# Key-key and query-key products of the first phase: plain fp32 products of 128 columns, or split products of 256

## The chip, the core and the metric

The kernel runs on one core of a Trainium2 chip. TensorE multiplies, VectorE and ScalarE work element by element, GpSimd does a few small things, and SyncE issues all DMAs of this kernel. The metric is the device time of one execution in microseconds, as the median of several runs. A profile is of one execution of its own, whose time stands beside it below.

## The reference

One layer of a hybrid backbone: 128 context tokens and 2048 latent tokens of 1024 features, thus 17 tiles of 128 tokens. The part that matters here is the front of the mixer, a gated DeltaNet with 4 heads of 128 features:

```python
proj = h @ w_in_l
qkv = jax.nn.silu(centred_conv(qkv, conv_l))
q, k, v = jnp.split(qkv, 3, axis=-1)
q = l2norm(q.reshape(B, T, H_A, DK))
k = l2norm(k.reshape(B, T, H_A, DK))
...
a_mat = jnp.where(strict, jnp.einsum('bnhcd,bnhsd->bnhcs', k_beta, k) * decay, 0.0)
...
qk = jnp.einsum('bnhcd,bnhsd->bnhcs', q, k) * decay
```

For each tile and head, k times k and q times k are needed, both 128 x 128, in fp32 accuracy. The scan over the chunks, the gMLP half, the output projection and the MLP follow.

## The kernel before

The program is written in phases. The first one (about the first 437 us) makes the normalised and modulated rows, projects them to q, k and v, convolves, and leaves in DRAM what the second phase (the scans and the gMLP, to about 1180 us) reads. The rest is the MLP.

The first phase walks over six blocks of tiles, five of three tiles and one of two (`BLOCKS`, line 28). In each block there are twelve feature tiles: k, q and v for each of four heads. The loop that begins with `for n, (gi, h) in enumerate(order)` gives each feature tile one slot. The main work of a slot is eight steps of `project`: three matmuls each, on the high and low parts of weights and rows (`mm3`, lines 241 to 243, 386 columns in most blocks). Between them `interleave` puts the side work of the slot, among it:

- `convolve` (lines 568 to 578), which leaves the features in the tile `x2`;
- `to_tokens` (lines 584 to 607), which transposes a feature tile; for k it also normalises the rows to `kn`, and for v it copies them to `tk`;
- `to_features` (line 614), which transposes `kn` back to `kTt`;
- `products` (lines 619 to 630), once for each head and block, three slots after the later one of its k and q tiles; 24 calls in all;
- steps of the modulation of later layers' parts (`mod_steps`), and of the next block's preparation (`prep_block`).

A matrix product that must be as exact as fp32 is done in one of two ways here. The plain way is a matmul on fp32 operands, which the program issues as two instructions (in the profile, 136 instructions stand for 68 products). The split way rounds each operand to the reduced type `F32R` (high part), takes the difference from it (low part), and adds up three matmuls: high with high, high with low and low with high. `products` uses the plain way before, `project` the split way.

Two things set the order of the work. The program's order gives each instruction a priority; a scheduler then lays out each engine's instructions in advance, from estimated times, so that an instruction whose inputs or buffers are not expected yet is passed by. On the chip each engine then runs its own list strictly as it was laid out. All stores and loads go through the one queue of SyncE.

Buffers come from pools. Tiles of one tag share as many buffers as `bufs` says, of the size of the largest; a new tile waits until the oldest is no longer used. The tags that the change touches: `first` holds the sums of the modulation (`mod_sum`, line 353, used four times in the first 40 us and read by the transposes of `mod_out`, line 361); `tk` holds `tk`, `kn` and, before, `ev`, the copy of the products out of PSUM; `xh` holds ten rows at the borders of blocks, read in the first 27 us. PSUM results of `to_tokens`, `to_features` and `products` share the three banks of `pt`.

Of the kernel before, what the change touches and what calls it, by code (L numbers as in the profile page):

```python
# [8 lines left out]
F32 = mybir.dt.float32  # L9
F32R = mybir.dt.float32r  # L10
# [3 lines left out]
ALU = mybir.AluOpType  # L14
# [3 lines left out]
P = 128  # L18
# [46 lines left out]
def hybrid_step(  # L65
# [7 lines left out]
    V, A, G, T = nc.vector, nc.scalar, nc.gpsimd, nc.tensor  # L73
    load = nc.sync.dma_start
    store = nc.sync.dma_start
# [10 lines left out]
    def f32(ap):  # L86
        return ap.bitcast(F32)
# [12 lines left out]
    kk_d = dp.tile([NT, P, H, P], F32, name="kk_d")  # L100
    qk_d = dp.tile([NT, P, H, P], F32, name="qk_d")
# [6 lines left out]
    def by_tiles(dst, tiles):  # L108

        return dst[tiles].rearrange("a p d -> p a d")  # L110
# [126 lines left out]
    def mm3(ps, trip, first=True, last=True, more=False):  # L237

        n = len(trip)
        for i, (lh, ll, rh, rl) in enumerate(trip):  # L240
            T.matmul(ps, lh, rh, start=first and i == 0, stop=False, skip_group_check=more)  # L241
            T.matmul(ps, lh, rl, start=False, stop=False, skip_group_check=more)  # L242
            T.matmul(ps, ll, rh, start=False, stop=last and i == n - 1, skip_group_check=more)  # L243
# [51 lines left out]
    with ExitStack() as ph:  # L295
        p1 = ph.enter_context(tc.tile_pool(name="p1", bufs=2, reuse_waits="tile"))
        pf = ph.enter_context(tc.tile_pool(name="p1f", bufs=2, reuse_waits="tile"))
# [6 lines left out]
        def pt():  # L304
            return ppt.tile([P, 512], F32, tag="pt", name="pt", bufs=3)
# [7 lines left out]
        for d in range(2):  # L313
            m = p1.tile([P, P], F32, tag=f"mcum{d}", name=f"mcum{d}", bufs=1)
# [9 lines left out]
        st_ = smp.tile([P, 16], F32, tag="c16", name="c16")  # L324
# [23 lines left out]
        def mod_sum(raws, psum):  # L348

            pm = psum()  # L350
            for k in range(KT):
                T.matmul(pm[0:2, :], scond[:, k, :], raws[k], start=k == 0, stop=k == KT - 1)
            row = pf.tile([2, 512], F32, tag="first", name="first", bufs=2)
            A.copy(row, pm[0:2, :])
            return row

# [52 lines left out]
        xh = pf.tile([P, D], F32, tag="xh", name="xh", bufs=1)[0:10, :]  # L409
# [7 lines left out]
        ps = pt()  # L417
# [4 lines left out]
        for t in BLOCKS[0]:  # L422
            x = p1.tile([P, D], F32, tag="x", name="x", bufs=3)
# [120 lines left out]
        def feature_tile(blk, bi, gi, h):  # L544

            hH, hL, ncol, segs = blk
            tiles = BLOCKS[bi]
            nt = len(tiles)
            n = nt * P
            c0 = tiles[0] * P  # L550
            j = gi * 4 + h
            u = {}

            def project(k):
                if k == 0:
                    u["ps"] = (pt if bi == 0 and j == 6 else pj)()
                wh, wl = W1[gi][k]
                mm3(u["ps"][:, :ncol], [(wh[:, h * P : (h + 1) * P], wl[:, h * P : (h + 1) * P],
                                         hH[k][:, :ncol], hL[k][:, :ncol])], first=k == 0, last=k == KT - 1)
                if k == KT - 1:  # L560
                    convolve()

            def convolve():
                ps = u["ps"]
                cv = pf.tile([P, 384], F32, tag="cv", name="cv", bufs=2)
                u["x2"] = x2 = pf.tile([P, 384], F32, tag="x2", name="x2", bufs=4)
                for s, o, m, _ in segs:
                    A.activation(cv[:, o : o + m], ps[:, s : s + m], AF.Copy, scale=convw[:, 1, j : j + 1])  # L568
                for s, o, m, _ in segs:
                    for w, sh in ((0, -1), (2, 1)):  # L570
                        V.scalar_tensor_tensor(out=cv[:, o : o + m], in0=ps[:, s + sh : s + sh + m],  # L571
                                               scalar=convw[:, w, j : j + 1], in1=cv[:, o : o + m],
                                               op0=ALU.mult, op1=ALU.add)
                A.activation(x2[:, :n], cv[:, :n], AF.Tanh, scale=0.5)
                V.scalar_tensor_tensor(out=x2[:, :n], in0=x2[:, :n], scalar=1.0, in1=cv[:, :n], op0=ALU.add,
                                       op1=ALU.mult)
                if gi == 0:
                    store(out=by_tiles(qT_d[:, :, h, :], slice(tiles[0], tiles[0] + nt)),
                          in_=x2[:, :n].rearrange("p (a d) -> p a d", d=P))

            def to_tokens():
                pq = pt()
                for i in range(nt):
                    T.transpose(pq[:, i * P : (i + 1) * P], u["x2"][:, i * P : (i + 1) * P], ident)  # L584
                rows = slice(c0, c0 + n)
                if gi == 2:
                    tk = pf.tile([P, 3, P], F32, tag="tk", name="tk", bufs=4)
                    A.copy(tk[:, :nt, :], pq[:, :n].rearrange("p (a b) -> p a b", b=P))
                    store(out=vt_d[rows, h * P : (h + 1) * P].rearrange("(a p) d -> p a d", p=P),
                          in_=tk[:, :nt, :])  # L590
                    return
                junk = p1.tile([P, P], F32, tag="junk2", name="junk2", bufs=1)
                if gi == 0:
                    for i, t in enumerate(tiles):
                        A.activation(junk, pq[:, i * P : (i + 1) * P], AF.Square,
                                     accum_out=ssq[:, t, h : h + 1])
                    return
                ss = smp.tile([P, 3], F32, tag="ss3", name="ss3")
                rk = smp.tile([P, 3], F32, tag="rk", name="rk")
                for i in range(nt):  # L600
                    A.activation(junk, pq[:, i * P : (i + 1) * P], AF.Square, accum_out=ss[:, i : i + 1])  # L601
                rsqrt_cols(rk[:, :nt], ss[:, :nt], nt, 1.0, 4 * EPS)
                u["kn"] = kn = pf.tile([P, 3, P], F32, tag="tk", name="kn", bufs=4)
                for i in range(nt):
                    A.activation(kn[:, i, :], pq[:, i * P : (i + 1) * P], AF.Copy, scale=rk[:, i : i + 1])
                store(out=kt_d[rows, h * P : (h + 1) * P].rearrange("(a p) d -> p a d", p=P),
                      in_=kn[:, :nt, :])

            def to_features():

                u["kTt"] = kTt = pf.tile([P, 384], F32, tag="kTt", name="kTt", bufs=3)
                pk = pt()
                for i in range(nt):
                    T.transpose(pk[:, i * P : (i + 1) * P], u["kn"][:, i, :], ident)
                V.tensor_copy(kTt[:, :n], pk[:, :n])
                store(out=by_tiles(kT_d[:, :, h, :], slice(tiles[0], tiles[0] + nt)),
                      in_=kTt[:, :n].rearrange("p (a d) -> p a d", d=P))

            def products(q):

                kTt = u["kTt"]
                for dst, rhs in ((kk_d, kTt), (qk_d, q["x2"])):
                    ps = pt()
                    for i in range(nt):
                        T.matmul(ps[:, i * P : (i + 1) * P], kTt[:, i * P : (i + 1) * P],  # L625
                                 rhs[:, i * P : (i + 1) * P], start=True, stop=True)
                    ev = pf.tile([P, 3, P], F32, tag="tk", name="ev", bufs=4)
                    A.copy(ev[:, :nt, :], ps[:, : nt * P].rearrange("p (a b) -> p a b", b=P))
                    store(out=dst[tiles[0] : tiles[0] + nt, :, h, :].rearrange("a p d -> p a d"),
                          in_=ev[:, :nt, :])  # L630

            u["main"] = [lambda k=k: project(k) for k in range(KT)]
            u["to_tokens"] = to_tokens
            u["to_features"], u["products"] = to_features, products
            return u
# [156 lines left out]
        for bi in range(len(BLOCKS)):  # L792
# [8 lines left out]
            for n, (gi, h) in enumerate(order):  # L801
                u = us[n] if bi == 0 and n < 3 else feature_tile(blk, bi, gi, h)
# [157 lines left out]
    with ExitStack() as ph:  # L960
# [465 lines left out]
        for i, u in enumerate(units):  # L1426
            w = p2 if i <= NT else p3
# [7 lines left out]
            n = len(u["prep"])  # L1435
# [6 lines left out]
            if i >= NT:  # L1442
                at(i, lambda u=u: o_loads(u))
                first, second = o_steps(u)
# [76 lines left out]
    def bank():  # L1521
        return psq.tile([P, 512], F32, tag="f", name="f", bufs=8)
# [356 lines left out]
    tiles = {n: [] for n in range(8)}  # L1879
# [49 lines left out]
    for j, t in enumerate(range(8, -1, -1)):  # L1929
        st = h2_steps(t, bank, lambda: w512("junk"), w512)  # L1930
        p = 10 + 19 * j // 2
# [7 lines left out]
    for p, (o, n, b) in enumerate(seq):  # L1939
        u = units[n]  # L1940
# [27 lines left out]
    for m, (n, i, u, q) in enumerate(todo):  # L1968
# [6 lines left out]
        if q == 0:  # L1975
            ps = bank()
# [6 lines left out]
        h, lo = sops.pop(m)  # L1983
        if m >= len(todo) - 4:
# [8 lines left out]
            if q == 3:  # L1993
                rest[0](ps, 0)
                ps = bank()
# [75 lines left out]
```

## Time and profile before

| | |
|---|---|
| runs | 2576.24, 2578.61, 2585.0 us; median 2578.61 |
| profiled execution | 2580.59 us, of it a span of 2578.7 us |
| TensorE's granted clock | 0.997 of full |
| plain products, line 625 | 272 matmul instructions, 38.3 us busy with overlap |
| copies of them, line 628 | 48 on ScalarE, 21.6 us |
| stores of them, line 629 | 48, of 192 KB (128 KB in the last block) |

The page of the profile gives the busy time of each engine and the chain of work that ended last. The views by windows, by lines and by time are answers of the same trace. Matmuls overlap: one may last 0.28 us though the next starts after 0.12. What a matmul costs is therefore read from the distance of starts, or from the chain, where each is charged only up to the next.

### The profile page before, as it was taken

The numbers are of one execution on the slowest core, as the hardware profiler recorded it, in microseconds if no ns is written. First come the engines' busy times: TensorE is split into PE (matmuls) and PEld (weight loads), VectorE is DVE, ScalarE is ACT, GpSimd is POOL, SyncE is SP. The second block draws the span as 40 slices with busy tenths as digits, with TensorE's granted clock in tenths as the row PEclk, the third lists the DMA queues.
The fourth block names the chain that finished last, engine by engine and source line by source line (L and its number), as shares of the span: only waits on it lengthen the run. The fifth ranks groups of instructions, "written<-read, shape, count | busy, mean of one in ns | idle before, by whom it ended". The sixth has DMA issues, their size and how long they took to land.

```text
span 2578.7 us, 44496 instructions
## 1 busy us (share of the span) xinstructions
PE 2539.4 (98%) x15268; PEld 2139.2 (83%) x15268; DVE 1836.7 (71%) x3790; ACT 1259.7 (49%) x3119; POOL 234.2 (9%) x448
## 2 busy tenths in 40 slices
PE   9999999999999999999999999999999999999998
PEld 5999999788888787778888888888888888888887
DVE  5867757776677878886677876777675557685875
ACT  4755556555555667764355543544442433243442
POOL 3112212111111111210000000000000000000000
PEclk9999999999999999999999999999999999999999
DMA  8967737644454657885768789666579979786683
GB/s 293 307 209 216 209 111 256 225 158 153 145 156 159 214 165 243 277 274 176 281 204 257 231 270 358 194 181 188 148 248 370 331 273 330 259 259 205 221 264 113
DMA packets 503912, 588.66 MB, mean 228 GB/s; under 512 B 36148, under 2 KB 298588, under 8 KB 500102
## 3 DMA queue, kind: packets, MB, share of 16 engines
q1 hardware_dynamic: 503686, 585.82, 69.6%
q8 instruction: 120, 1.97, 0.3%
q14 instruction: 106, 0.87, 0.1%
HBM read 406.01 MB, written 179.67 MB: 227 GB/s over the span
## 4 chain that ended last, share of the span: by engine, by line
PE 89%; DMA 5%; DVE 4%; ACT 1%; issue 1%; POOL 0%; SPq 0%; POOLq 0%; DVEq 0%; ACTq 0%
PE f L241 17%; PE f L242 17%; PE f L243 17%; PE pj L241 7%; PE pj L243 7%; PE pj L242 7%; PE pd L1010 5%; PE pm L241 1%; PE pm L243 1%; PE pm L242 1%; DMA raw<-in_w_mod_dram 1%; PE pt L625 1%; PE pt L584 1%; PE pd L1093 1%; DMA hop_d<-opL 1%
## 5 line engine op out<-in xcount | busy, mean ns | idle before, releaser
L241 PE MATMUL f<-hop,zH 128*128 128x512 f32 (+1 forms) x976 | 376.2, 386 | 1.2 <-ACT zH L1531 1.2
L242 PE MATMUL f<-hop,zH 128*128 128x512 f32 (+1 forms) x976 | 376.1, 386 | 0.0
L243 PE MATMUL f<-hop,zL 128*128 128x512 f32 (+1 forms) x976 | 376.1, 386 | 0.0
L241 PE MATMUL f<-hop,wH 128*128 128x512 f32 x896 | 349.7, 391 | 0.6 <-ACT p L1604 0.6
L242 PE MATMUL f<-hop,wH 128*128 128x512 f32 x896 | 348.7, 389 | 0.0
L243 PE MATMUL f<-hop,wL 128*128 128x512 f32 x896 | 347.5, 389 | 0.0
L1531 ACT CAST zH<-zraw 128x512 fp32r<-128x512 f32 x240 | 146.9, 620 | 302.4 <-DMA zraw<-s_d 93.6
L241 PEld LDWEIGHTS f<-hop,zH 128*128 128x128 f32 x976 | 183.3, 188 | 38.6 <-ACT zH L1531 1.6
L243 PEld LDWEIGHTS f<-hop,zL 128*128 128x128 f32 x976 | 183.3, 188 | 37.3 <-DVE zL L1525 0.4
L242 PEld LDWEIGHTS f<-hop,zH 128*128 128x128 f32 x976 | 183.3, 188 | 36.9 <-issue 0.2
L1525 DVE TENSOR_TENSOR zL<-zraw,zH 128x512 fp32r<-128x512 f32 x240 | 163.2, 687 | 66.5 <-ACT zH L1531 54.0
L241 PEld LDWEIGHTS f<-hop,wH 128*128 128x128 f32 x896 | 168.2, 188 | 36.5 <-ACT p L1604 1.7
L243 PEld LDWEIGHTS f<-hop,wL 128*128 128x128 f32 x896 | 168.2, 188 | 35.3
L242 PEld LDWEIGHTS f<-hop,wH 128*128 128x128 f32 x896 | 168.3, 188 | 34.5
L241 PE MATMUL pj<-kH,wH 128*128 128x386 f32 (+2 forms) x568 | 190.5, 338 | 1.3 <-ACT junk L601 1.1
L243 PE MATMUL pj<-kH,wL 128*128 128x386 f32 (+2 forms) x568 | 189.7, 335 | 0.0
L242 PE MATMUL pj<-kL,wH 128*128 128x386 f32 (+2 forms) x568 | 189.5, 335 | 0.1
L184 POOL TENSOR_TENSOR r<-rsq,nhalf 128x1 f32<-128x1 f32 (+1 forms) x37 | 25.7, 694 | 1409.0 <-DVE rsq L183 1409.0
L571 DVE SCALAR_TENSOR_TENSOR cv<-pj,vec,cv 128x384 f32<-128x384 f32 (+2 forms) x164 | 87.0, 539 | 53.4 <-ACT cv L568 52.0
L1531 ACT CAST wH<-s 128x512 fp32r<-128x512 f32 x96 | 59.4, 621 | 124.6 <-DVE s L1525 118.3
L241 PEld LDWEIGHTS pj<-kH,wH 128*128 128x128 f32 x568 | 107.1, 189 | 4.4 <-issue 2.4
L202 DVE TENSOR_TENSOR wL<-raw,wH 128x512 fp32r<-128x512 f32 x120 | 81.7, 688 | 40.0 <-ACT wH L201 36.6
(418 smaller groups left out, 5806.9 us busy)
## 6 DMA issues: line engine op xcount, KB each, us to landing
zraw<-z_d SPq DMA_DIRECT2D x212, 256.0 KB
raw<-in_w_ff_dram SPq DMA_DIRECT2D x192, 256.0 KB
hop<-hop_d SPq DMA_DIRECT2D x28, 1024.0 KB
z_d<-c SPq DMA_DIRECT2D x96, 256.0 KB
zraw<-s_d SPq DMA_DIRECT2D x96, 256.0 KB
raw<-in_w_mod_dram SPq DMA_DIRECT2D x80, 256.0 KB
r<-in_w_ff_dram SPq DMA_DIRECT2D x80, 256.0 KB
s_d<-s SPq DMA_DIRECT2D x64, 256.0 KB
```

The costliest lines, as they stand in the source:

```text
L184: G.tensor_tensor(out=out, in0=t[:np_, :n], in1=nhalf[:np_, :n], op=ALU.pow)
L202: V.tensor_tensor(out=lo, in0=raw, in1=f32(h), op=ALU.subtract)
L241: T.matmul(ps, lh, rh, start=first and i == 0, stop=False, skip_group_check=more)
L242: T.matmul(ps, lh, rl, start=False, stop=False, skip_group_check=more)
L243: T.matmul(ps, ll, rh, start=False, stop=last and i == n - 1, skip_group_check=more)
L571: V.scalar_tensor_tensor(out=cv[:, o : o + m], in0=ps[:, s + sh : s + sh + m], scalar=convw[:, w, j : j + 1], in1=cv[:, o : o + m], op0=AL ...
L584: T.transpose(pq[:, i * P : (i + 1) * P], u["x2"][:, i * P : (i + 1) * P], ident)
L625: T.matmul(ps[:, i * P : (i + 1) * P], kTt[:, i * P : (i + 1) * P], rhs[:, i * P : (i + 1) * P], start=True, stop=True)
L1010: T.matmul(p[:, h, :], lhs[:, h, :], rhs[:, h, :], start=True, stop=True)
L1093: T.matmul(py[:, h], u["X"][:, h, :], pm[:, h], start=True, stop=True)
L1525: V.tensor_tensor(out=out, in0=a, in1=b, op=op)
L1531: A.copy(h, src)
```

## The change

`products` changes from the plain to the split way, and the moving operand of a tile now holds k's columns and q's columns together, 256 in all. The high parts of both go into one tile `kqH` (under the tag `xh`), made on ScalarE; the low parts go into `kqL`, made on VectorE, which takes the buffer of tag `first`. For each tile of tokens, the stationary operand is the high part of k (twice) and its low part (once). Two tiles of tokens fill one PSUM bank, so a call on three tiles uses one bank of 512 columns and one of 256, as against two banks of 384. One copy per bank brings them to `ev`, a tile of its own with one buffer that holds both results of the call; then come the two stores. The row tag `first` and the tag `tk` each lose one buffer (2 to 1 and 4 to 3).

```diff
-            row = pf.tile([2, 512], F32, tag="first", name="first", bufs=2)
+            row = pf.tile([2, 512], F32, tag="first", name="first", bufs=1)
...
-                    tk = pf.tile([P, 3, P], F32, tag="tk", name="tk", bufs=4)
+                    tk = pf.tile([P, 3, P], F32, tag="tk", name="tk", bufs=3)
...
-                u["kn"] = kn = pf.tile([P, 3, P], F32, tag="tk", name="kn", bufs=4)
+                u["kn"] = kn = pf.tile([P, 3, P], F32, tag="tk", name="kn", bufs=3)
...
             def products(q):
 
-                kTt = u["kTt"]
-                for dst, rhs in ((kk_d, kTt), (qk_d, q["x2"])):
+                hi = pf.tile([P, 2, 384], F32R, tag="xh", name="kqH", bufs=1)
+                lo = pf.tile([P, 2, 384], F32R, tag="first", name="kqL", bufs=1)
+                for w, x in enumerate((u["kTt"], q["x2"])):
+                    A.copy(hi[:, w, :n], x[:, :n])
+                    V.tensor_tensor(out=lo[:, w, :n], in0=x[:, :n], in1=f32(hi)[:, w, :n], op=ALU.subtract)
+                ev = pf.tile([P, 2, 3, P], F32, tag="ev", name="ev", bufs=1)
+                for i0 in range(0, nt, 2):
+                    m = min(2, nt - i0)
                     ps = pt()
-                    for i in range(nt):
-                        T.matmul(ps[:, i * P : (i + 1) * P], kTt[:, i * P : (i + 1) * P],
-                                 rhs[:, i * P : (i + 1) * P], start=True, stop=True)
-                    ev = pf.tile([P, 3, P], F32, tag="tk", name="ev", bufs=4)
-                    A.copy(ev[:, :nt, :], ps[:, : nt * P].rearrange("p (a b) -> p a b", b=P))
-                    store(out=dst[tiles[0] : tiles[0] + nt, :, h, :].rearrange("a p d -> p a d"),
-                          in_=ev[:, :nt, :])
+                    for i in range(m):
+                        c = slice((i0 + i) * P, (i0 + i + 1) * P)
+                        out = ps[:, i * 256 : i * 256 + 256].rearrange("p (w d) -> p w d", w=2)
+                        for j, (st_, mv) in enumerate(((hi, hi), (hi, lo), (lo, hi))):
+                            T.matmul(out, st_[:, 0, c], mv[:, :, c], start=j == 0, stop=j == 2)
+                    A.copy(ev[:, :, i0 : i0 + m, :].rearrange("p w a d -> p a w d"),
+                           ps[:, : m * 256].rearrange("p (a w d) -> p a w d", a=m, w=2))
+                for w, dst in enumerate((kk_d, qk_d)):
+                    store(out=dst[tiles[0] : tiles[0] + nt, :, h, :].rearrange("a p d -> p a d"), in_=ev[:, w, :nt, :])
```

## The prediction

> **What bounds the kernel now.** I began with the page, whose busy shares and chain of waits name the engine that sets the end.
>
> ```profile
> span 2578.7 us, 44496 instructions
> PE 2539.4 (98%) x15268; PEld 2139.2 (83%) x15268; DVE 1836.7 (71%) x3790; ACT 1259.7 (49%) x3119; POOL 234.2 (9%) x448
> PE 89%; DMA 5%; DVE 4%; ACT 1%; issue 1%; POOL 0%; SPq 0%; POOLq 0%; DVEq 0%; ACTq 0%
> ```
>
> TensorE is on 89% of the chain. But the change touches only the first phase (up to about 437 us), so the second view is the table of windows, in stretches that follow the blocks of that phase.
>
> ```profile
> core 0: us, PE busy (x) PEld busy (x) DVE busy (x) ACT busy (x) POOL busy (x), PEclk, DMA share, GB/s
> 40.00:110.00 70.00, 68.01 (x403) 65.27 (x401) 55.41 (x141) 49.92 (x140) 18.03 (x42) 1.00 0.88 281
> 110.00:175.00 65.00, 64.05 (x418) 62.16 (x418) 51.15 (x99) 39.73 (x128) 5.44 (x13) 1.00 0.86 267
> 175.00:240.00 65.00, 65.00 (x408) 62.77 (x408) 42.77 (x85) 35.20 (x108) 13.06 (x33) 1.00 0.65 189
> 240.00:300.00 60.00, 60.00 (x387) 57.73 (x386) 44.16 (x89) 33.12 (x103) 11.85 (x37) 1.00 0.68 202
> 300.00:365.00 65.00, 65.00 (x413) 63.26 (x412) 41.08 (x83) 33.08 (x104) 12.98 (x37) 1.00 0.53 153
> 365.00:440.00 75.00, 75.00 (x543) 71.80 (x542) 47.70 (x130) 43.81 (x131) 18.50 (x21) 1.00 0.66 200
> sum 400.00, PE 397.06 PEld 382.99 DVE 282.27 ACT 234.86 POOL 79.85; mean PE 66.18 PEld 63.83 DVE 47.05 ACT 39.14 POOL 13.31
> ```
>
> From 175 us on TensorE never stops: what it is given there is what the phase takes, and a microsecond of matmul removed is a microsecond gained. Before 175 us it stops for 2.94 us (70.00 - 68.01 and 65.00 - 64.05), with the DMA engines at 0.88 and VectorE at 55.41 of 70. A finer set of windows shows where VectorE is full:
>
> ```profile
> 90.00:100.00 10.00, 10.00 (x67) 9.78 (x66) 8.00 (x18) 6.20 (x21) 0.38 (x1) 1.00 1.02 312
> 100.00:110.00 10.00, 10.00 (x61) 9.72 (x59) 7.08 (x16) 7.38 (x19) 6.99 (x30) 1.00 1.01 323
> 110.00:120.00 10.00, 9.05 (x61) 8.60 (x61) 9.97 (x19) 6.10 (x23) 0.44 (x4) 1.00 1.06 351
> ```
>
> From 90 us the DMA engines are full, and from 110 to 120 us VectorE has nothing left. The first block's products fall just here.
>
> **TensorE's sum.** The old products are 24 calls (6 blocks by 4 heads). A call has two products of 128 columns for each tile, and each is two instructions. The view by line and form counts them; the chain gives what each call really costs, because there each matmul is charged only until the next can start.
>
> ```profile
> L625 PE MATMUL pt<-kTt 128*128 128x128 f32 x136 | 19.2, 275 | 0.8 <-ACT junk L595 0.8
> L625 PE MATMUL pt<-x,kTt 128*128 128x128 f32 x136 | 19.1, 275 | 0.0
> 233.36 1.34 PE pt L625 x12
> 413.26 0.89 PE pt L625 x8
> ```
>
> A call on three tiles costs 1.34 us, on two tiles 0.89 us (0.112 us an instruction, not the 275 ns that one of them lasts: they overlap). 20 x 1.34 + 4 x 0.89 = 30.4 us.
>
> The new call has per tile three matmuls with 256 moving columns of the reduced type (high with high, high with low, low with high): 9 or 6 instead of 12 or 8. Such matmuls are the last ones of the kernel, 17 in a row, of which the first and the last:
>
> ```profile
> 2569.72 0.28 PE L242 MATMUL f<-hop,zH 128*128 128x256 f32 x1
> 2571.64 0.28 PE L243 MATMUL f<-hop,zL 128*128 128x256 f32 x1
> ```
>
> 16 steps in 1.92 us: 0.120 us each. 20 x 9 x 0.120 + 4 x 6 x 0.120 = 24.5 us. **TensorE saves 30.4 - 24.5 = 5.9 us**, 0.23% of the time. It is little because a plain fp32 product of 128 columns takes 2 x 0.112 = 0.223 us, while its share of three 256-column matmuls takes 3 x 0.120 / 2 = 0.180 us.
>
> The Trainium skill puts this differently: "TensorE: Matmul & The Clock Gate" (Back-to-back issue gap) gives N / 2.4 + 2.5 ns, 109 ns for 256 columns. By that, as an estimate, the new matmuls would take 22.2 us and the saving would be 8.1 us. The rows above show 120 ns in this kernel, and I go by them.
>
> One form the trace does not have: the moving operand is two runs of 128 columns, 384 apart. It could cost as little as the unbroken row (0.120 us), and at the far end as much per column as the plain products (0.447 us for 256 columns, four times 0.112). I take 0.120, since it has the type and width of that row and differs only by one jump.
>
> **ScalarE and VectorE.** Their new work is not on the chain, but TensorE now has to wait for it.
>
> ```profile
> L628 ACT COPY ev<-pt 128x384 f32<-128x384 f32 x40 | 18.7, 481 | 15.5 <-PE pt L625 14.4 <-DMA kk_d<-ev 0.8 <-DMA qk_d<-ev 0.2
> L628 ACT COPY ev<-pt 128x256 f32<-128x256 f32 x8 | 2.9, 372 | 0.5 <-PE pt L625 0.4
> L201 ACT CAST wH<-raw 128x512 fp32r<-128x512 f32 x51 | 30.5, 633 | 7.9 <-DMA raw<-in_w_in_dram 4.6 <-DMA raw<-in_w_mod_dram 3.2
> L202 DVE TENSOR_TENSOR wL<-raw,wH 128x512 fp32r<-128x512 f32 x50 | 33.3, 682 | 4.2 <-ACT wH L201 3.6 <-PE pj L243 0.3
> L520 DVE TENSOR_TENSOR kL<-full,kH 128x256 fp32r<-128x256 f32 x8 | 3.3, 418 | 0.0
> ```
>
> - Evictions: two of 384 columns become one of 512 and one of 256 (481 + 109 = 590 and 372 ns, the slope from the first two rows). 962 ns before and after; on the last block one of 590 for two of 372. Nothing to speak of.
> - High parts: two casts a call on ScalarE. From the cast of 512, less 109 ns, 0.52 us for 384 columns: 40 x 0.52 + 8 x 0.42 = 24 us.
> - Low parts: two subtractions a call on VectorE. Midway between 418 and 682 ns, 0.55 us: 40 x 0.55 + 8 x 0.42 = 25 us.
>
> Over 40 to 440 us VectorE goes from 282 to 308 of 400 (77%), ScalarE from 235 to 259 (65%). In sum there is room: TensorE's stream covers both. If that cover is gone, a call costs up to its whole preparation, two casts and the last subtraction, 0.52 + 0.52 + 0.55 = 1.6 us.
>
> The inputs are old: k's transposed tile and q's features are made well ahead of the call, since a call is put three tiles after its later one. So the casts can run early; but the single buffers for high and low let them start only when the call before has ended. The chain shows calls 4.5 us apart (233.36 above and the next two), so 4.5 - 1.1 = 3.4 us stay for the 1.6 us of preparation.
>
> ```profile
> 237.87 1.34 PE pt L625 x12
> 242.38 1.34 PE pt L625 x12
> ```
>
> **Moved and shared.** The stores stay 48, of the same size, but both of a call leave after the second eviction, from one buffer, and the next call's first eviction waits until both have landed. The trace shows one such store on the chain, at the end of the phase:
>
> ```profile
> 437.60 4.79 DMA vt_d<-tk
> ```
>
> 4.79 us for a store in full traffic against 4.5 us between calls: the eviction can be late by about 1 us where DMA is full. Queued behind it on ScalarE are the copies, tanh and squares of the next tile; ScalarE is idle 35% of the time, and TensorE has three PSUM banks for these results, so I cost it at nothing; uncovered it is at most 1 us on the calls of the two blocks before 175 us, some 8 us. On SP's queue a waiting store holds back the loads behind it in the same way as now; the first store of a call moves back by about 0.4 us of matmuls and the second eviction. The three buffers left to kn and tk lose one and are rid of 48 of 96 users: nothing. The modulation rows, now one buffer:
>
> ```profile
> 11.87 0.58 ACT L354 COPY first<-pm 2x512 f32<-2x512 f32 x1 [9.06 <-PE pm L352]
> 19.16 0.57 ACT L354 COPY first<-pj 2x512 f32<-2x512 f32 x1 [6.72 <-PE pj L352]
> 16.05 0.41 PE L361 MATMUL pm<-ident,first 2*128 2x2 f32 x4
> 24.20 0.41 PE L361 MATMUL pm<-ident,first 2*128 2x2 f32 x4
> 28.44 0.56 ACT L354 COPY first<-pj 2x512 f32<-2x512 f32 x1
> ```
>
> Each copy already comes after the transposes that read the row before it (19.16 after 16.46, 28.44 after 24.61): one buffer costs nothing.
>
> **What of the saving is kept.** In the first block it meets a transfer that does not come earlier:
>
> ```profile
> 99.04 5.34 DMA raw<-in_w_mod_dram
> 110.98 0.94 PE L625 MATMUL pt<-kTt 128*128 128x128 f32 x6 [0.81 <-ACT junk L595]
> ```
>
> The chain leaves TensorE for a load at 99 us and comes back with a wait of 0.81 us. What its four calls save, 4 x 0.26 = 1.0 us, I take as lost. For new waits on high or low parts I take one more of that 0.81 us, its bounds being none and 24 x 1.6 = 38 us; it lies near none because the phase after 175 us shows not one stop, although transposes there read VectorE's results too. **-5.9 + 1.0 + 0.8 = about -4.0 us**: 2580.6 (the profiled execution: its span and 1.9 us around it) becomes 2576.6. It lies 2.0 us above the median of the runs, 2578.6; so the forecast for the median is **2574.6 us**.
>
> **The rivals.**
> - *Faster, 2568 us (0.20).* The instructions of each engine stand in an order that is laid out from estimated times, so the phase behind can come out in another order. It has slack worth having:
>
> ```profile
> 496.56 4.76 DMA S<-in_state_delta_dram
> 501.46 2.50 PE pd L1010 x16
> 524.88 1.78 PE pd L1010 x16
> ```
>
> TensorE stops for the state's load and then runs 16 matmuls in 2.50 us that later take 1.78. If the load came early, 4.76 + 0.72 = 5.5 us go as well, and with all of the 5.9 kept the sum is -11 us. Against it: nothing in the change aims there, and such luck has two signs.
> - *All of it eaten, 2577 to 2584 us (0.14).* ScalarE's or VectorE's queue is late in the first two blocks only (windows at 9.97 of 10): 8 calls x 0.8 to 1.2 us is 6.4 to 9.6 us against 5.9, or the late stores above.
> - *Slower, 2592 us (0.16).* TensorE waits for the low parts at every call: the subtraction stands in VectorE's queue behind convolutions and modulation sums. The price is that of the wait at 110.98 us: 24 x 0.81 = 19.4, less 5.9, +13.5 us. It decides for slower by more than 0.3% from a mean wait of (5.9 + 7.7) / 24 = 0.57 us a call. For it: VectorE at 79% before 175 us; against it: 3.4 us of room for 1.6 us. The Trainium skill, "TensorE: Matmul & The Clock Gate" (its table's row on queue depth), says that ScalarE and VectorE take their instructions strictly in order; that speaks for this rival, and the wait above, for squares that other squares held back, agrees.
> - *It does not do what it says:* the broken moving operand runs at the far end, 204 x 0.447 = 91 us, +61 us, 2639 us. Only as a share of the slower cases (0.02 of the 0.16), for the reason above.
>
> **How the numbers follow.** The forecast's own case (from the full -5.9 to about -1) has 0.50. 0.3% is 7.7 us, about what a measurement can tell from no change here; so it and the eaten case are "same", 0.64; faster 0.20, slower 0.16. For 8 in 10 the range takes in half of the faster case, to 2567, and reaches half way into the slower one, to 2588.
>
> **What would show it.** Right: the line of the products takes about 1.1 us a call in the chain (x9, or x6 and x3), the windows after 175 us have TensorE full over a shorter stretch, about 1 us less a block. Wrong: waits on the high or low parts in the list of waits of TensorE; a step of the new matmuls above 0.13 us; evictions waiting for stores with TensorE idle behind them; or a second phase whose own span differs by more than 2 us, which no term here covers.

## The result and the profile after

| | before | after |
|---|---|---|
| median of the runs (22 each) | 2578.93 us (2575.43 to 2585.0) | 2584.22 us (2578.08 to 2591.23) |
| profiled execution | 2580.59 us, span 2578.7 | 2582.28 us, span 2580.5 |
| TensorE's granted clock, mean of the runs | 0.9984 (29 other runs of before, those of the first group) | 0.9961 |

The ratio is 1.0021, with an interval of 1.0014 to 1.0028: the change makes the kernel 5.3 us **slower**. It lies inside the range and within 0.3%, but the forecast was 4 us faster. The two profiled executions are only 1.7 us apart, since before's lies above the median of its runs and after's below; the medians decide, and the table's last line will help to say why.

The page of the kernel after, its span, busy times and chain:

```profile
span 2580.5 us, 44424 instructions
PE 2534.8 (98%) x15200; PEld 2133.4 (83%) x15200; DVE 1857.9 (72%) x3838; ACT 1273.0 (49%) x3163; POOL 242.0 (9%) x448
PE 82%; DMA 7%; DVE 6%; ACT 2%; SPq 1%; issue 1%; POOL 0%; POOLq 0%; DVEq 0%; ACTq 0%
```

TensorE is busy 4.6 us less than before (2539.4), and yet the span is longer: time went from matmuls into waits, and the chain has more DMA and DVE than it had. The table of windows says where:

```profile
40.00:110.00 70.00, 68.14 (x401) 65.33 (x399) 57.99 (x147) 51.16 (x145) 18.96 (x33) 1.00 0.87 273
110.00:175.00 65.00, 61.12 (x368) 59.17 (x368) 53.42 (x106) 38.98 (x127) 8.14 (x18) 0.95 0.81 250
175.00:240.00 65.00, 65.00 (x412) 62.79 (x411) 48.44 (x97) 36.50 (x108) 13.70 (x37) 1.00 0.69 198
...
365.00:440.00 75.00, 75.00 (x540) 72.03 (x539) 54.02 (x143) 47.17 (x138) 17.16 (x21) 1.00 0.66 201
```

For TensorE only the row of 110 to 175 us differs much: it is idle for 3.88 us (before 0.95), with a granted clock of 0.95. From 175 us on TensorE is full as before. Of the list of TensorE's waits from 40 to 475 us, the rows of the two places where it changed, first of before, then of after (total, times, longest):

```profile
PE pm L243 <- DMA hL<-hL_d: 1.0, 1, 1.0
PE pt L625 <- ACT junk L595: 0.8, 1, 0.8
```

```profile
PE pt L634 <- ACT junk L595: 3.2, 1, 3.2
PE pm L241 <- DMA hH<-hH_d: 2.9, 1, 2.9
PE pj L241 <- POOL kH L509: 1.1, 2, 0.7
```

Two small stops became two long ones: one in the new products at the end of the first block, one on the first rows `hH` of the second phase. Neither is a wait for the high or low parts of the products (`kqH`, `kqL`). The last row is new, a wait for the next block's rows; every other row of the two lists is 1.1 us or less.

To place gains and losses I set the start of the n-th matmul of line 241 beside that of before (worked out from the instructions of the trace; negative is sooner):

| start before, us | 107.2 | 128.6 | 144.1 | 391.9 | 425.0 | 442.6 | 463.9 | end |
|---|---|---|---|---|---|---|---|---|
| after minus before, us | -1.2 | +4.8 | +4.8 | +0.8 | -0.8 | 0.0 | +3.5 | +1.8 |

Read from left to right: the first products gain; **the end of the first block loses 5.9 us; the blocks behind it gain 5.6; the border to the second phase loses 4.3**.

**The matmuls themselves.** The timeline of TensorE in the first block of after (start, duration):

```profile
103.23 0.28 PE L634 MATMUL pt<-kqL,kqH 128*128 128x256 f32 x1
103.35 0.28 PE L634 MATMUL pt<-kqH,kqL 128*128 128x256 f32 x1
```

Their step is 0.12 us, the value that the prediction took. ScalarE's casts and VectorE's subtractions (ns: least, median, most), by the view of the tile of high parts:

```profile
L624 ACT CAST kqH<-x x24: 397/521/606, 76.5 to 428.7; 128x384 fp32r<-128x384 f32 x20, 128x256 fp32r<-128x256 f32 x4
L625 DVE TENSOR_TENSOR kqL<-x,kqH x24: 418/553/560, 77.1 to 429.2; 128x384 fp32r<-128x384 f32 x20, 128x256 fp32r<-128x256 f32 x4
```

521 and 553 ns stand against forecasts of 520 and 550.

**The stop in the first block.** The chain of waits of after, from 105 us:

```profile
105.06 0.60 DVE kL L529
105.66 0.47 DVE x L575
106.16 0.23 DVE cv L571
106.39 6.49 DMA x<-in_x_sample_dram
112.96 1.15 ACT junk L467 x2
114.11 0.26 ACT junk L595 x2
114.57 0.20 ACT junk L595
114.82 2.29 PE pt L634 x9
```

From the bottom: the products at 114.82 wait for the squares of the transposed q tile (L595, which free the PSUM bank); these stand on ScalarE behind the squares of the next block's row (L467); these wait for the row; and the row's load left SyncE only at 106.39. In before the last two of these loads left together, the last one at 102.3 us, 4 us sooner (timeline of SyncE):

```profile
101.66 0.97 SPq L462 DMA_DIRECT2D x<-in_x_sample_dram  x2
```

In after four other transfers stand between the two in SyncE's list:

```profile
103.34 0.38 SPq L462 DMA_DIRECT2D x<-in_x_sample_dram  x1
103.81 0.38 SPq L534 DMA_DIRECT2D hL_d<-kL  x1
104.29 0.44 SPq L256 DMA_DIRECT2D raw<-in_w_mod_dram  x1
104.82 0.41 SPq L534 DMA_DIRECT2D hH_d<-kH  x1
105.33 0.97 SPq L256 DMA_DIRECT2D raw<-in_w_mod_dram  x1
106.39 0.52 SPq L462 DMA_DIRECT2D x<-in_x_sample_dram  x1
```

So the late thing is a transfer, and it is late because of what now stands ahead of it in SyncE's list. That it is VectorE's subtractions that change this order is argued, but all traces fit it. In the five kernels that make these subtractions on VectorE in the first block and have the row's squares in their old place (after, and four of the kernels below), the same four transfers stand between the two loads, and TensorE loses 4.0 to 5.9 us from 107.2 to 128.6 us. In the five kernels below that keep the first block plain with the squares in place, and in the one with the low parts on GpSimd, the two loads leave together, and it loses 1.5 us at most. Behind the stop the timeline of TensorE shows what no term of the prediction had:

```profile
114.82 0.58 PE L634 MATMUL pt<-kqH 128*128 128x256 f32 x1 [3.19 <-ACT junk L595]
115.19 0.42 PE L634 MATMUL pt<-kqL,kqH 128*128 128x256 f32 x1
115.41 0.41 PE L634 MATMUL pt<-kqH,kqL 128*128 128x256 f32 x1
...
120.12 0.53 PE L242 MATMUL pj<-kL,wH 128*128 128x386 f32 x1
120.44 0.53 PE L243 MATMUL pj<-kH,wL 128*128 128x386 f32 x1
120.77 0.39 PE L241 MATMUL pj<-kH,wH 128*128 128x386 f32 x1
120.99 0.34 PE L242 MATMUL pj<-kL,wH 128*128 128x386 f32 x1
```

After 3.19 us of rest the matmuls step by 0.22 instead of 0.12 us and by 0.32 instead of 0.18, until about 120.8; the clock record of the trace has half clock for 6.8 us, from 114.0 to 120.9, of which 6.0 us lie behind the stop. The block's end costs its added idle time (3.88 - 0.95 = 2.9 us) and half of these 6.0 us: 5.9 us, and the table shows 5.9. The Trainium skill, "TensorE: Matmul & The Clock Gate" (Part 1: The HAM clock gate), says that the clock falls to half after an idle window of about 3.4 us, and that these windows run freely; the lengths in the trace agree (6.8 us here, 3.4 behind the stop at the border), but the stops before them were shorter, 3.19 and 2.95 us.

It bears on the table's last line too: 0.9984 - 0.9961 = 0.0023 of the clock, times 2580, is 5.9 us that the runs of after lose more at half clock than those of before, as much as the matmuls were to save. Runs of the same granted clock are much alike: at 0.996, 0.997 and 0.998 the runs of after (8, 4 and 4) have means of 2585.0, 2580.4 and 2581.5 us, those of before beside the experiments (3, 19 and 44) 2584.8, 2581.7 and 2579.4. So most of the 5.3 us between the medians goes with the clock. The two profiles can't show it, because both executions hold 10.2 us at half clock: after in the windows of 6.8 and 3.4 us behind the two stops, before in three of 3.4 us in the later phases (from 502.8, 892.0 and 915.9 us).

### The profile page after: what moved, and what is told of

It is laid out like the page before. It is cut to its first block, busy times and chain, and to the rows that moved or that the text cites. A ratio compares the mean times of both kernels' runs of the same rounds, so it can differ in the third digit from the quotient of the medians.

```text
span 2580.5 us, 44424 instructions
## 1 busy us (share of the span) xinstructions
PE 2534.8 (98%) x15200; PEld 2133.4 (83%) x15200; DVE 1857.9 (72%) x3838; ACT 1273.0 (49%) x3163; POOL 242.0 (9%) x448
## 4 chain that ended last, share of the span: by engine, by line
PE 82%; DMA 7%; DVE 6%; ACT 2%; SPq 1%; issue 1%; POOL 0%; POOLq 0%; DVEq 0%; ACTq 0%
PE f L243 15%; PE f L241 15%; PE f L242 15%; PE pj L241 7%; PE pj L243 7%; PE pj L242 7%; PE pd L1018 5%; PE pm L241 1%; PE pm L243 1%; PE pm L242 1%; DMA raw<-in_w_ff_dram 1%; DMA QK<-qk_d 1%; PE pt L634 1%; DMA raw<-in_w_mod_dram 1%; PE pt L584 1%
## 5 line engine op out<-in xcount | busy, mean ns | idle before, releaser
L241 PEld LDWEIGHTS pj<-kH,wH 128*128 128x128 f32 x568 | 107.7, 190 | 5.5 <-POOL kH L509 1.9
L242 PEld LDWEIGHTS pj<-kL,wH 128*128 128x128 f32 x568 | 108.0, 190 | 1.3 <-issue 0.7
```

## The experiments

Fourteen kernels were timed, one of them twice, in four groups; each group shares its runs of before (2578.99, 2579.59, 2578.65 and 2580.19 us). Diffs are against the kernel after unless something else is said.

### First group: which part of the change costs

**The first block plain, the others split.** In place of the three dots: before's two plain loops, copied into the halves of `ev`, and then both stores.

```diff
             def products(q):
+                if bi == 0:
...
+                    return
```

> The first block's four calls are plain again, all else as after the change. Theory A: the loss is one stop of TensorE at the end of the first block (3.2 us at 112 to 115 us, with half the clock behind it), because VectorE's subtractions there delay the reader of the x buffers, so the next rows load late, their squares stand at the head of ScalarE's list, and the squares behind them hold the PSUM banks. Then the stop falls back to about 0.8 us and the five other blocks keep about 1 us each: 4 us below the kernel before, about 2575 us. Theory B: the single buffer of ev and the late stores cost time everywhere: about 5 us above before, as after the change. Theory C: small waits spread over all calls: a sixth of the loss goes, about 4 us above before.

2581.21 us, 1.0008 (0.9999 to 1.0018): 3 us less than after. The stop of 3.2 us is gone, the blocks behind gain as in after (-4.8 at 425 us against before), but the border takes nearly all of it back (-0.4 at 463.9). Its list of waits has, as in after:

```profile
PE pm L241 <- DMA hH<-hH_d: 2.7, 1, 2.7
```

So two places lose, and to mend one isn't enough. Theory A's 2575 us did not come, and theories B and C, 4 to 5 us above before, are too high: it is 2.2.

**Plain products everywhere, with after's buffers and stores.**

```diff
-                hi = pf.tile([P, 2, 384], F32R, tag="xh", name="kqH", bufs=1)
-                lo = pf.tile([P, 2, 384], F32R, tag="first", name="kqL", bufs=1)
...
+                for w, (dst, rhs) in enumerate(((kk_d, kTt), (qk_d, q["x2"]))):
                     ps = pt()
+                    for i in range(nt):
+                        T.matmul(ps[:, i * P : (i + 1) * P], kTt[:, i * P : (i + 1) * P],
+                                 rhs[:, i * P : (i + 1) * P], start=True, stop=True)
+                    A.copy(ev[:, w, :nt, :], ps[:, : nt * P].rearrange("p (a b) -> p a b", b=P))
```

> The matmuls of before in all blocks, with the buffers and the two stores behind the second eviction of after (ev as one tile with one buffer, tk with three, the modulation's row with one). Theory A: within 2 us of before, no stop above 1 us in the first phase. Theory B: 6 to 11 us above before, since the waits are there and the saving of 5.9 us is not. Theory C: within 2 us of before.

2582.67 us, 1.0013 (1.0003 to 1.0023). Nothing of the arithmetic is changed, and it is 3.7 us slower than before: TensorE is 3.6 us late at 128.6 us, and the border adds 2.1. "Nothing" was the wrong price for buffers and the place of stores; the 3.7 us lie between what the theories expected. Whether that is the single buffer itself or any new order, the last group takes up.

**Low parts on GpSimd**, to relieve VectorE.

```diff
-                    V.tensor_tensor(out=lo[:, w, :n], in0=x[:, :n], in1=f32(hi)[:, w, :n], op=ALU.subtract)
+                    G.tensor_tensor(out=lo[:, w, :n], in0=x[:, :n], in1=f32(hi)[:, w, :n], op=ALU.subtract)
```

> As after, with the low parts made on GpSimd in place of VectorE, in all blocks. Theory A: VectorE has its old load, the stop at 112 us falls to 1 us or less, and the time is about 4 us below before (2575 us), unless GpSimd's subtractions are longer than 1.5 us each. Theory B: as after, 5 us above before. Theory C: lies with the casts on ScalarE, so as after too; if with VectorE, some us below it.

2590.64 us, 1.0047 (1.0033 to 1.0061): the worst of all. The stop in the first block shrinks to 1.5 us, but at the border the timeline of GpSimd shows

```profile
424.58 11.25 POOL L184 TENSOR_TENSOR rq<-rsq,nhalf 128x68 f32<-128x68 f32 x1 [1.12 <-DVE rsq L183]
435.79 0.74 POOL L625 TENSOR_TENSOR kqL<-kTt,kqH 128x256 fp32r<-128x256 f32 x1
```

The last call's low parts stand behind a power of 11.25 us, and `hH` is waited for 8.8 us. The time says much about the queue that the work moved to. The first block says something about VectorE: without the subtractions there the last two row loads leave SyncE together again (at 104.6 and 105.1 us), and TensorE loses 1.5 us from 107.2 to 128.6 us instead of 5.9.

**The squares of the row (L467) moved into the next step of the norm**, so that they no longer stand ahead of L595.

```diff
-                A.activation(junk, x, AF.Square, accum_out=xs[0][:, i : i + 1])
+                rows_in.append((i, x))
...
-                first += [lambda: (columns_r(), load_pair(0)), lambda: (rows_r(), load_pair(1)), lambda: load_pair(2)]
+                first += [lambda: (squares(), columns_r(), load_pair(0)), lambda: (rows_r(), load_pair(1)), lambda: load_pair(2)]
```

> As after, with the squares of the next block's three row tiles put one to three slots later, in one step with the norm that needs them, so that they do not stand in ScalarE's list while their loads are under way. Theory A: TensorE no longer stops for squares at the end of the first block, though the rows come as late: about 4 us below before. Theory B and C: as after, about 5 us above before.

2580.10 us, 1.0003 (0.9994 to 1.0011): 4.1 us less than after. The long stop on L595 goes, and others come at the same place:

```profile
PE pj L241 <- DVE ab L671: 2.2, 1, 2.2
PE pm L241 <- DMA hH<-hH_d: 1.6, 1, 1.6
...
PE pt L640 <- ACT junk L601: 1.3, 1, 1.3
PE pt L640 <- DVE kqL L631: 0.7, 1, 0.7
```

The first block still ends 3.5 us late, and theory A's 4 us below before did not come. The squares were the last link of the chain, not its cause: from 100 to 130 us VectorE is busy 28.01 of 30 us in this run (before 25.17, after 25.56), and with the squares away TensorE waits 2.2 us for one of its results.

### Second group: the border

I supposed that the last calls' stores, held up by the single `ev`, delay the loads behind them on SyncE.

**The last block's calls one slot sooner**, alone and with the squares moved; **before with the squares moved**, as the control of the latter; **the last block's results in buffers of their own**.

```diff
-                    if n == max(at[1, hh], at[0, hh]) + 3:
+                    if n == max(at[1, hh], at[0, hh]) + (3 if nxt else 2):
```

> As after, but the last block's four calls stand two slots after their later tile in place of three. Theory D: besides the first block, the border to the second phase eats the gain: the one ev buffer makes each eviction of the last block wait until the stores before it have landed, so the last stores leave some 5 us late, the loads of these products for the second phase wait for them on SyncE's queue, and the rows that TensorE needs stand behind these loads (a stop of 2.9 us, and half the clock behind it). Then the last stores leave 3 us sooner, the stop is below 1 us, and the time is 3 to 4 us below after: about 2580.5 us. Rival E (the border's stop is an accident of one execution or of the order): as after, about 2584 us.

> The squares later (as in the run before) and the last block's calls one slot sooner, together. Theory D: both losses are cut, about 2576 to 2577 us, 2 to 3 us below before. Rival E: no better than the squares alone, about 2580 us.

> The kernel before with the squares later, without the change. Theory A: before stops only 0.8 us for such squares, so within 1.5 us of before (2579 us). If the squares are worth as much to before as they were to after (4 us), what they removed was no cost of the change: about 2575 us.

```diff
-                ev = pf.tile([P, 2, 3, P], F32, tag="ev", name="ev", bufs=1)
+                if bi == len(BLOCKS) - 1:
+                    evs = [p1.tile([P, 388], F32, tag="h", name="evh", bufs=24)[:, :n].rearrange("p (a d) -> p a d", d=P) for _ in range(2)]
+                else:
+                    ev = pf.tile([P, 2, 3, P], F32, tag="ev", name="ev", bufs=1)
+                    evs = [ev[:, w] for w in range(2)]
```

> As after, but in the last block ev is taken from tiles that are free there (those of the next block's rows, which the last block does not prepare), so that no eviction waits for a store; the copies of a call are two of 256 columns there. Theory D: the last stores leave about 4 us sooner, the border's stop falls below 1 us, and the time is 3 to 4 us below after: about 2580.5 us. Rival E: as after, about 2584 us.

| kernel | median us | ratio | stop on `hH`, us | last stores issued at, us |
|---|---|---|---|---|
| after | 2584.22 | 1.0021 (1.0014 to 1.0028) | 2.9 | 436.28, 436.72 |
| sooner | 2585.34 | 1.0025 (1.0014 to 1.0036) | 4.4 | 434.53, 434.96 |
| sooner, squares moved | 2579.61 | 1.0001 (0.9991 to 1.0011) | 2.9 | 428.89, 429.32 |
| before, squares moved | 2580.99 | 1.0007 (0.9998 to 1.0015) | none | |
| own buffers | 2585.0 | 1.002 (1.0012 to 1.0029) | 4.8 | 436.46, 436.93 |

The supposition **falls**. With the last stores 7.4 us sooner the stop is the same 2.9 us; with buffers of their own it is longer, and the stores leave no sooner. The squares' move helps the split kernel by 4 us and does not help before (+1.4 to its own before, an interval that takes in none), so it doesn't look like a better order for all.

### Third group: the results back in the tag `tk`, and which blocks are split

Here each call's two results are tiles of the tag `tk` again, which gets five buffers, with four evictions to a call; then the first block plain (`bi in (0,)` in the second diff); then the first and the last plain; and that with the squares moved.

```diff
-                ev = pf.tile([P, 2, 3, P], F32, tag="ev", name="ev", bufs=1)
+                evs = [pf.tile([P, 3, P], F32, tag="tk", name="ev", bufs=5) for _ in range(2)]
...
+                    p4 = ps[:, : m * 256].rearrange("p (a w d) -> p a w d", a=m, w=2)
+                    for w in range(2):
+                        A.copy(evs[w][:, i0 : i0 + m, :], p4[:, :, w, :])
```

```diff
+                if bi in (0, 5):
...
+                    return
```

> As after, but the two copies of a call out of PSUM are tiles of their own again, from the buffers of tk (five, of the space that after gives to ev and tk), so a call's evictions no longer wait for the one buffer of the call before. Theory B: what the buffers alone cost (3.7 us) comes back: about 2580.5 us. If not the buffer but the order and the engines' new work lose the time, as after: about 2584 us.

> The same, with the first block's calls plain as before. Theory F (the loss is in stops of TensorE at the end of the first block and at the border to the second phase, each with half the clock behind it): about 2578 us, with the granted clock near 0.997. If blocks two to six lose too: 2580 or more.

> The same, with the first and the last block plain as before; only blocks two to five are split, where the windows show TensorE without a stop. Theory F: neither stop grows, 16 calls save 0.26 us each: 4 us below before, about 2575 us, clock 0.998. Rival G (the border is bound by its transfers, so what TensorE gains ahead of it is given back there): no better than before, 2579 us, with a stop of TensorE at the border as long as the gain.

> The same with the squares later. Theory F: as the run before, within 1.5 us, since the first block is that of before. Rival G: the same as well.

| split blocks (of six) | median us | ratio |
|---|---|---|
| all | 2581.86 | 1.001 (1.0001 to 1.0018) |
| all but the first | 2581.61 | 1.0008 (0.9999 to 1.0017) |
| **the four in the middle** | **2572.38** | **0.998 (0.9967 to 0.9992)** |
| the four in the middle, squares moved | 2576.59 | 0.9996 (0.9985 to 1.0007) |

The third is the first kernel that beats before, by 6.3 us; theory F had 4, and rival G, that nothing would be gained, falls. The fourth is 4.2 us above the third, where 1.5 at most was expected. That the squares' move costs there is not shown, since the intervals overlap and the third, timed again below, came out at 2575.64.

### Fourth group: is it the split, and which end costs what

> Plain products in all six blocks, with the other buffers of the kernel that splits only the four middle blocks: five buffers of tag tk, one row of tag first. Nothing is left out. Theory S (the 6 us of that kernel come from the split matmuls of the middle blocks): this one stands at the time before, ratio 0.999 to 1.001, and TensorE between 140 and 410 us gains nothing on before. Rival T (they come from the five buffers or from another laid-out order): ratio 0.998 or below, 2573 us.

> The kernel that splits only the four middle blocks, once more and beside its control. Nothing is left out. If its gain is real: 2570 to 2576 us, ratio 0.997 to 0.9995, and at least 3 us below the kernel with plain products and the same buffers. If it was one lucky measurement: ratio 0.9995 to 1.001, within 2 us of that kernel.

> Five blocks split, only the last plain, ev from five buffers of tag tk. Nothing is left out. It tells apart the two places of the loss. If the last block is what makes the border to the second phase late: the wait for the first high part of hH is at most 1 us, as before, and the ratio is 0.999 to 1.0005, worse than that of the four middle blocks alone only by the loss at the end of the first block (3 to 5 us). If the first block alone costs, the wait at the border is 3 us or more although the last block is plain, and the ratio is 1.000 to 1.002.

The kernels are that of the third group with `bi in (0, 1, 2, 3, 4, 5)`, `(0, 5)` once more, and `(5,)`.

| split blocks (of six) | median us | ratio | shift at 144.1 | at 391.9 | at 463.9 |
|---|---|---|---|---|---|
| none | 2583.60 | 1.001 (0.9998 to 1.0023) | +1.0 | +1.0 | +4.2 |
| the four in the middle | 2575.64 | 0.9984 (0.9969 to 0.9998) | -0.1 | -5.1 | -5.5 |
| the first five | 2584.65 | 1.0015 (1.0004 to 1.0025) | +6.3 | +3.2 | +5.0 |

The shifts are the starts of line 241's matmuls against before in the profiled executions, at before's times. The gain is real: it comes a second time, and the control with the same buffers and plain products has none of it (the two medians of this group are 8.0 us apart). Between 144 and 392 us, four split blocks gain 5.0 us, the control 0.0; 16 calls at 0.26 us would be 4.2. The first five gain 3.1 there, and after 4.0. The first five fit neither forecast whole: TensorE waits 1.3 us for `hH`, where one had at most 1 and the other at least 3, and the kernel is worse than the four middle blocks by more than the 3 to 5 us that the first block was to cost.

**The first block.** Between the last two rows only its four calls differ, and they cost 2584.65 - 2575.64 = 9.0 us (each interval is some 3 us to either side). That holds with the last block plain; with the last block split, the first two rows of the third group differ by 0.3 us. TensorE's waits from 100 to 130 us, with the first block split and with it plain:

```profile
PE pt L646 <- ACT junk L595: 1.8, 2, 1.6
PE pj L241 <- POOL kH L509: 1.4, 1, 1.4
```

```profile
PE pt L626 <- ACT junk L595: 0.7, 1, 0.7
```

The last of the three row loads leaves SyncE at 107.7 us with the first block split and at 101.3 with it plain (after: 106.4, before: 102.3); that moves with the first block alone, and the stops follow it. With it split, the four transfers shown above stand again between the second and the third load.

**The last block.** In the third group, between "all but the first" and "the four in the middle", only its four calls differ: 2581.61 - 2572.38 = 9.2 us. The timeline of SyncE, last block split:

```profile
438.60 0.48 SPq L1048 DMA_DIRECT2D kt<-kt_d  x1
439.12 0.51 SPq L1046 DMA_DIRECT2D kT<-kT_d  x1
440.26 1.40 SPq L1036 DMA_DIRECT2D KK<-kk_d  x2
441.72 0.89 SPq L1040 DMA_DIRECT2D QK<-qk_d  x2
442.66 0.90 SPq L1259 DMA_DIRECT2D hH<-hH_d  x2
```

and plain, in the repeated run of the four middle blocks:

```profile
433.80 1.10 SPq L1036 DMA_DIRECT2D KK<-kk_d  x2
434.99 0.44 SPq L1276 DMA_DIRECT2D gate_d<-th  x1
435.49 1.43 SPq L1040 DMA_DIRECT2D QK<-qk_d  x2
437.32 0.33 SPq L190 DMA_DIRECT2D raw<-in_w_in_dram  x1
437.72 0.89 SPq L1259 DMA_DIRECT2D hH<-hH_d  x2
```

TensorE is 3.9 and 5.1 us ahead of before at 412 us, so nearly alike, but `hH` is issued 4.9 us later in the former, with loads of `kt` and `kT` laid out ahead of it, and TensorE waits 4.3 us for it, against 1.0 us (for `hL`) in the latter. That the last block's split makes the border late is shown where the first block is plain; **by which link is open**. Late stores and the single buffer did not account for it in the second group. The loads of `kt` and `kT` can't be all of it, for in the kernel "sooner, squares moved" none stands ahead of `hH` and the stop is 2.9 us. The control with plain products everywhere also lost 3.2 us at the border in its profile (+1.0 to +4.2). A kernel that fixes SyncE's order by hand was not tried.

The two ends don't add up (difference to its before in us, `ev` in `tk`: all six split +3.2, all but the first +3.0, all but the last +4.5, the middle four -6.3 and -4.5): either end alone costs what both do. The likely reading is that what the first block has lost the border does not take a second time, since there TensorE waits for a time that SyncE sets; with all six split it waited 1.3 us for `hH` instead of 4.3.

## Why the prediction was wrong

- **What bounds the kernel: right where TensorE is full, and there alone.** From 144 to 392 us a microsecond less of matmul was about a microsecond gained (5.0 us with plain ends, 4.0 in after, 3.1 with the first five split, against 4.2 by the prediction's terms). At the two ends the phase is set by row loads and by SyncE's list.
- **TensorE's sum, -5.9: right.** A step of 0.12 us; the blocks behind the first gain 5.6 us in after, against 4.9 by the prediction's terms without the first block (16 x 0.26 + 4 x 0.17). The broken moving operand costs nothing more.
- **ScalarE and VectorE: the durations right, the cover wrong.** It was judged by sums (77% of VectorE) and by the room between calls. TensorE did not wait for the products' high or low parts in after; what came late with the new work was the next block's row load, through the order of SyncE's list. VectorE's busy time does not tell the two apart: from 110 to 120 us it is 9.97 of 10 in after as in before.
- **"+1.0 for the first block" and "+0.8 for waits": the step that failed.** The first block lost 5.9 us and the border 4.3. Mis-sized were two things: the length of the stops (3.2 and 2.9 instead of one more 0.81), and what hangs on a stop: a window at half clock, which cost 3.0 us behind the first. The profile of before had it: the 2.50 us for 16 matmuls that later took 1.78 (its clock record has half clock from 502.8 to 506.3 us), which the prediction counted in a rival as a bonus, and not as the price of every new stop.
- **Buffers and stores "at nothing": failed.** Plain products with after's buffers cost 3.7 us, and with five buffers of `tk` 3.4 (its interval just takes in none). As two unlike sets of buffers cost the same, the single `ev` alone isn't the cause; that any new laid-out order may cost so much is the reading that is left, and two runs don't settle it. `ev` back in `tk`, with all blocks split, gave 2.4 us (2584.22 to 2581.86, of different groups, with intervals that overlap).
- **The rivals.** The nearest is "all of it eaten", 2577 to 2584, for late queues in the first blocks: right about the place, 0.2 us short at its end, and without the border. "Slower" by waits for low parts at every call did not come. Of the signs of failure none came in after's profile: the step is 0.12 us, and the second phase from 442.6 to 1180 us is 1.6 us shorter as a whole, though it loses 3.5 us in its first 21. The list of signs had no entry for a late load.

In sum for after, in its profile: -1.2, +5.9, -5.6, +4.3 and -1.7 behind 463.9 us is +1.7. Of the -1.7, -2.6 falls between 500 and 510 us, where before's execution waited longer for a load (1.9 us, after 0.8) and then had one of its windows at half clock. The other 3.6 of the medians' 5.3 are not in this profile; the runs' lower granted clock would cover them, but where in those executions it fell has no record.

## What to carry to other kernels

Price a stop of TensorE with the half clock behind it, and look for stops at the ends of a phase, where loads set the pace, before spending saved matmul time there: the same change in only the four blocks where TensorE is full gained 4.5 to 6.3 us, and in all six lost 3.2 with the same buffers and 5.3 with those of after. When the forecast gain is 0.2%, run the same buffers with the old arithmetic beside it: here the two such controls alone moved by 3.4 and 3.7 us.

## What was not expected of the hardware

- Half clock lasted 3.4 us or a multiple of it (6.8, once 10.2), and short stops sufficed: 1.36 and 1.59 us within 4 us of each other in the kernel with five split blocks. From 68 to 76 us it came in some profiled executions and not in others: stops of 1.04, 0.85 and 0.91 us had 6.8 us at half clock with them (the four middle blocks' first run), stops of 1.67, 0.38 and 1.13 us none (plain products with after's buffers). So the length of the stops does not settle it. That a kernel with more stops draws half clock more often would fit the mean clocks (0.9984 before, 0.9961 after, 0.9945 with the low parts on GpSimd), but no run shows it.
- Moving 128 + 128 columns from two places 384 apart costs TensorE no more than 256 in one run (0.12 us).
- A power on GpSimd over 128x68 took 11.25 us, in before as well, and the subtraction behind it in the list started only when it ended (435.79 us).
